# A diffusion block on one core: the row root and the feature gemv at the kernel's front, rearranged

## The chip, the cores and the metric

The kernel runs on one core of one Trainium2 chip. The metric is the device time of one execution in microseconds. Before the change the median of three runs is 1590.12 us (1589.61 to 1594.4).

## What is computed

One block of a diffusion backbone works on 256 latent tokens `x` and 256 context tokens `ctx`, each with 2048 features, in float32:

```python
lam = exp(sum(lp[0] * lp[1])) - exp(sum(lp[2] * lp[3])) + lam_init      # lp = da_lambda
mod   = silu(c) @ w_ada + b_ada         # latent: shift, scale, gate, twice
mod_c = silu(c_ctx) @ w_ada + b_ada     # context
h_lat = rmsnorm(x, norm1_g) * (1 + sc1) + sh1
h_ctx = rmsnorm(ctx, norm1_g) * (1 + csc1) + csh1
dq, dk, dv, cq, ckv, kr, ga, gb = split(h @ w_in)     # for h_lat and h_ctx
# differential attention (uses lam) and latent attention over 512 keys,
# their output projections, sigmoid gates, w_out, gated residual
# second norm and modulation, SwiGLU (2048 -> 5632 -> 2048), gated residual, final norm
```

## The kernel before

Matmul operands are split into a high and a low part (`fp32r`), and each product is three matmuls: high by high, low rows by high weights, high rows by low weights. ScalarE makes the high part of a weight tile (`wh`, L169), VectorE the low part (`wl`, L170); both kinds of tile share rings of three buffers, the raw tiles a ring of five.

The first stage, which the change touches, does this. `xnT` holds the 512 tokens as columns and the features in 16 k-tiles of 128. Eight transfers on SyncE's queue bring it. ScalarE squares each tile of 1024 columns (L320, L323), VectorE adds the squares into `xsum` (L324, seven adds), then adds its two halves (L325), and one matmul with a matrix of ones sums over the partitions (L327, into `ps`). `newton` (L305 to L312) makes the reciprocal root of the 512 sums: Ln, Exp and Square on ScalarE, three steps on VectorE. The result `rb` scales each k-tile of `xnT` (L370).

The shift and the scale of the first norm come from `w_mod`, the first two chunks of `w_ada`. `mod_gemv(f0, nf, order)` computes them for `nf` k-tiles of output features from `f0` on: SyncE loads `w_mod` in tiles of 512 KB (`sraw`, 12 buffers; four tiles for one k-tile, eight for two), 16 matmuls of 32 columns each, four of them side by side in the array, go into `pgb` (L390), ScalarE copies it to `res` (L383), TensorE transposes it (L386), VectorE reduces it to the columns `modc` (L397 to L404), and then the k-tiles' modulated rows are made: high part on ScalarE (L409), low part on VectorE (L410, L411). Behind that, `first_group(k0, nk)` loads the k-tiles' share of 832 columns of `w_in` (the MLA key and value compression, the rope key, and the first four heads' pairs of `dk`), splits it, and puts 42 feature matmuls for each k-tile into a `queue`: 7 banks (`g0`, numbers 0 to 6), six each.

Within `tc.manual_schedule` TensorE's order is the program's. The list `order` writes it: `"g4"` is four matmuls of the gemv, a number takes so many feature matmuls from the queue, `"t"` is the copy, eight feature matmuls and the transposes. On the other engines the framework's planner orders the instructions. The calls are

```python
mod_gemv(0, 1, ["g4", "g4", "g4", "g4", "t"])
mod_gemv(1, 1, [16, "g16", "t"])
mod_gemv(2, 2, [36, "g8", 4, "g8", "t"])
for f0 in range(4, KT, 2):
    mod_gemv(f0, 2, [len(queue) - 54, "g16", "t", 22])
pop(len(queue))
```

The last block's matmuls go bank by bank (0, 1, 5, 2, 3, 4, 6), all others go over the k-tiles with the banks in two parts (2, 3, 5 and 0, 1, 4, 6). Then the banks are evacuated: 0, 1, 4 and 6 are `dk` of the first four heads (`evac_dk`, rotary positions and split, VectorE L530 to L540), 2, 3 and 5 the MLA latents (`evac_latent`), while TensorE goes on with `dq` and `dv`. Banks 4 and 6 are read by the second pair of heads.

The lambdas (L273 to L287) stand ahead of all that: a transfer of 128 KB on ScalarE's queue into a buffer of the `wl` ring, two multiply-reduce steps, an Exp and two small steps. Their result `nlam` is read by the differential attention (L665).

Of the kernel before, what the change touches and what calls it, by code (L numbers as in the profile page):

```python
# [11 lines left out]
F32 = mybir.dt.float32  # L12
# [84 lines left out]
def kernel(  # L97
# [41 lines left out]
    def nm(s):  # L139
        uid[0] += 1  # L140
        return f"{s}{uid[0]}"
# [17 lines left out]
    def load_w(src, a, n):  # L159
        raw = stream.tile([P, 1024], F32, tag="raw", name=nm("raw"), bufs=5)  # L160
        nc.sync.dma_start(out=raw[:, : a * n], in_=src)
        return raw[:, : a * n].rearrange("p (a n) -> p a n", a=a)
# [54 lines left out]
    def group_b(w, c0, n, nkt, toks, name, ups=2, tick=None, stagger=0):  # L217
# [52 lines left out]
    b1 = const.tile([P, 16], F32, name="b1")  # L270
    nc.vector.tensor_scalar_add(b1, bcol[:, 16:32], 1.0)

    ls = const.tile([P, 4], F32, name="ls")  # L273
    setup = stream.tile([P, 1024], F32, tag="wl", name="setup", bufs=3)
    lamb, lj = setup[:, 0:256], setup[:, 512:576]
    nc.scalar.dma_start(
        out=lamb, in_=da_lambda.rearrange("a f d -> (a f d)").partition_broadcast(P))
    for i in range(2):
        nc.vector.tensor_tensor_reduce(
            lj, lamb[:, i * 128 : i * 128 + 64], lamb[:, i * 128 + 64 : i * 128 + 128],  # L280
            op0=ALU.mult, op1=ALU.add, scale=1.0, scalar=0.0, accum_out=ls[:, i : i + 1])
    with tc.issue_after(silu.ins):
        nc.scalar.preload_act_table_set("natural_log_exp_and_others")
    nc.scalar.activation(ls[:, 0:2], ls[:, 0:2], AF.Exp)
    nlam = ls[:, 2:3]
    nc.vector.tensor_sub(nlam, ls[:, 1:2], ls[:, 0:1])
    nc.vector.tensor_scalar_add(nlam, nlam, -LAM_INIT)  # L287


    right, close_right = pool("right", side="right")  # L290
# [4 lines left out]
    xnT = xp.tile([P, KT, 512], F32, name="xnT")  # L295
    c32 = xp.tile([P, KT, 32], F32, name="c32")
    nc.gpsimd.memset(c32, 0.0)
    nc.vector.tensor_copy(c32[:, :, 0:2], cols[:, 0:32].rearrange("p (v k) -> p k v", v=2))
    srp, close_sr = pool("srp", side="right")

# [4 lines left out]
    def newton(y, q, ps, n):  # L305

        nc.scalar.activation(y, ps, AF.Ln, bias=epsc, scale=1.0 / n)
        nc.scalar.activation(y, y, AF.Exp, scale=-0.5)
        nc.scalar.activation(q, y, AF.Square)
        nc.vector.scalar_tensor_tensor(q, ps, n * EPS, q, op0=ALU.add, op1=ALU.mult)  # L310
        nc.vector.tensor_scalar(q, q, -0.5 / n, 1.5, op0=ALU.mult, op1=ALU.add)
        nc.vector.tensor_mul(y, y, q)  # L312

    xsum = xp.tile([P, 1024], F32, name="xsum")
    for u in range(8):
        xu = xnT[:, 2 * u : 2 * u + 2, :]
        nc.sync.dma_start(out=xu, in_=xt[:, 2 * u : 2 * u + 2, :])
        xu = xu.rearrange("p a n -> p (a n)")
        if u == 0:
            nc.scalar.activation(xsum, xu, AF.Square)  # L320
        else:
            sq = stream.tile([P, 1024], F32, tag="wh", name=nm("sq"), bufs=3)
            nc.scalar.activation(sq, xu, AF.Square)  # L323
            nc.vector.tensor_add(xsum, xsum, sq)  # L324
    nc.vector.tensor_add(xsum[:, :512], xsum[:, :512], xsum[:, 512:])  # L325
    ps = acc(nm("ps"))
    nc.tensor.matmul(ps, ones, xsum[:, :512], start=True, stop=True)  # L327
    rb = xsum[:, :512]
    newton(rb, xsum[:, 512:], ps, D)

# [32 lines left out]
    def mod_gemv(f0, nf, order):  # L365

        for kt in range(f0, f0 + nf):
            nc.vector.tensor_mul(xnT[:, kt, :], xnT[:, kt, :], rb)  # L370
        w = nf * 256
        a = 4 // nf
        vs = []
        for u in range(KT // a):
            raw = srp.tile([P, 1024], F32, tag="sraw", name=nm("sraw"), bufs=SRAW)
            last_load[0] = nc.sync.dma_start(
                out=raw, in_=w_mod.block(u * a, a, f0 * P, nf * P, D + f0 * P, nf * P))
            vs += [raw[:, i * w : (i + 1) * w] for i in range(a)]
        done = 0
        for step in order:  # L380
            if step == "t":
                res = xp.tile([P, 512], F32, tag="res", name=nm("res"), bufs=1)
                nc.scalar.copy(res[:, :w], pgb[:, :w])  # L383
                pop(8)
                for j in range(2 * nf):
                    nc.tensor.transpose(pgb[:, j * P : (j + 1) * P], res[:, j * P : (j + 1) * P], ident)  # L386
            elif isinstance(step, str):
                for kt in range(done, done + int(step[1:])):
                    j = kt % 4
                    nc.tensor.matmul(pgb[32 * j : 32 * j + 32, :w], c32[:, kt, :], vs[kt],  # L390
                                     start=kt < 4, stop=kt >= 12, tile_position=(0, 32 * j))
                done += int(step[1:])
            else:
                pop(step)
        assert done == KT

        nc.vector.tensor_reduce(  # L397
            modr[:, :, :nf, :],
            pgb[:, : 2 * nf * P].rearrange("p (s i g v) -> p s i v g", s=2, i=nf, g=4)[:, :, :, 0:2, :],
            axis=AX.X, op=ALU.add)  # L400
        for i in range(nf):
            kt = f0 + i
            nc.vector.tensor_scalar(modc[:, kt, 0, :], modr[:, 0, i, :], bcol[:, kt : kt + 1], None, op0=ALU.add)
            nc.vector.tensor_scalar(modc[:, kt, 1, :], modr[:, 1, i, :], b1[:, kt : kt + 1],  # L404
                                    n1g[:, kt : kt + 1], op0=ALU.add, op1=ALU.mult)
            for v, hh in enumerate((hl, hc)):
                sh, sc = modc[:, kt, 0, v : v + 1], modc[:, kt, 1, v : v + 1]
                xv = xnT[:, kt, v * 256 : v * 256 + 256]
                nc.scalar.activation(hh[0][:, kt, :], xv, AF.Identity, bias=sh, scale=sc)  # L409
                nc.vector.tensor_scalar(xv, xv, sc, sh, op0=ALU.mult, op1=ALU.add)  # L410
                nc.vector.tensor_sub(hh[1][:, kt, :], xv, hh[0][:, kt, :].bitcast(F32))  # L411
        queue.extend(first_group(f0, nf))

    def first_group(k0, nk):

        v = load_w(w_in.block(k0, nk, 3584, 320), nk, 320)
        wh = stream.tile([P, 1024], F32R, tag="wh", name=nm("wh"), bufs=3)
        wl = stream.tile([P, 1024], F32R, tag="wl", name=nm("wl"), bufs=3)
        h1 = wh[:, : nk * 384].rearrange("p (a n) -> p a n", a=nk)
# [2 lines left out]
        nc.vector.tensor_sub(l1[:, :, :320], v, h1[:, :, :320].bitcast(F32))  # L422
        nc.scalar.copy(h1[:, :, 320:], h1[:, :, 256:320].bitcast(F32))
        nc.scalar.copy(l1[:, :, 320:], l1[:, :, 256:320].bitcast(F32))
        h2, l2 = split_w(load_w(w_in.block(k0, nk, 1024, 512), nk, 512), nk, 512)

        def cut(i, n):
            return (h1, l1)[i][:, :, n * P : (n + 1) * P] if n < 3 else (h2, l2)[i][:, :, (n - 3) * P : (n - 2) * P]
# [27 lines left out]
        return todo  # L456

    with tc.manual_schedule(engines={mybir.EngineType.PE}):
        mod_gemv(0, 1, ["g4", "g4", "g4", "g4", "t"])
        mod_gemv(1, 1, [16, "g16", "t"])  # L460
        mod_gemv(2, 2, [36, "g8", 4, "g8", "t"])
        for f0 in range(4, KT, 2):

            mod_gemv(f0, 2, [len(queue) - 54, "g16", "t", 22])
        pop(len(queue))
    with tc.issue_after(last_load[0].ins):
        nc.sync.dma_start(out=cst, in_=consts)
    close_sr()
# [541 lines left out]
```

## Time and profile before

| | |
|---|---|
| median of 3 runs | 1590.12 us (1589.61 to 1594.4) |
| profiled execution | 1599.08 us, its span 1597.3 us |
| TensorE, matmuls | 1541.9 us busy (97%) |
| VectorE | 1016.4 us (64%) |
| ScalarE | 737.4 us (46%) |
| GpSimd | 16.1 us (1%) |
| HBM read | 352.37 MB, 222 GB/s over the span |

The rows are of one execution taken by the hardware profiler. Times are microseconds from the start of the span unless marked ns. PE is TensorE, PEld its weight loads, DVE VectorE, ACT ScalarE, POOL GpSimd, SP SyncE; L327 is line 327 of the kernel. A window's row gives busy time and instructions of PE, PEld, DVE, ACT and POOL in that order, then the granted TensorE clock as a share of full speed (2.4 GHz), the busy share of the 16 DMA engines and the GB/s that they moved. A float32 matmul stands as two records. A matmul's end in the records includes the time until its result is out, so matmuls that follow each other overlap a little.

### The profile page before, as it was taken

The page shows a single profiled execution, that of the slowest core. Times are in us where ns is not written, and L with a number is a line of the kernel's source. Part 1 is how long each engine was busy: PE and PEld are TensorE (multiplying, and loading weights), DVE is VectorE, ACT ScalarE, POOL GpSimd, SP SyncE. Part 2 cuts the span into 40 slices and gives each one's busy share as a digit, 9 for nine tenths or more (in the row PEclk, how much of TensorE's full clock was granted, in tenths as well). Part 3 has the DMA queues.
Part 4 walks back from the last instruction along what each step waited for, and adds up shares of the span by engine and source line. Part 5 has one row for each costly group of instructions (what it writes and reads, how often), then busy time and mean ns, then how long its engine had stood idle before and what let it go on. Part 6 is the DMA issues. An engine that isn't in the chain of part 4 may idle for free.

```text
span 1597.3 us, 28864 instructions
## 1 busy us (share of the span) xinstructions
PE 1541.9 (97%) x11966; PEld 1445.0 (90%) x11966; DVE 1016.4 (64%) x1360; ACT 737.4 (46%) x1038; POOL 16.1 (1%) x14
## 2 busy tenths in 40 slices
PE   3899999998999999999999999999999999999997
PEld 2678899997889999999999999999999999888886
DVE  5437887787896667666776566767554554445454
ACT  4335455545675443444445444444444444344343
POOL 0000000000000000000000000000000000011010
PEclk9999999999999999999999999999999999999999
DMA  9894653456455787888884678888565656655663
GB/s 369 338 367 153 213 170 121 136 178 197 142 165 170 257 290 249 280 269 292 306 280 159 205 229 281 282 285 272 196 194 192 196 194 219 194 190 191 193 191 119
DMA packets 100594, 356.34 MB, mean 223 GB/s; under 512 B 10992, under 2 KB 13552, under 8 KB 100208
## 3 DMA queue, kind: packets, MB, share of 16 engines
q1 hardware_dynamic: 99600, 351.58, 65.9%
q10 hardware_dynamic: 864, 2.93, 0.6%
q8 instruction: 93, 1.52, 0.4%
q14 instruction: 37, 0.30, 0.1%
HBM read 352.37 MB, written 2.10 MB: 222 GB/s over the span
## 4 chain that ended last, share of the span: by engine, by line
PE 72%; DMA 9%; DVE 6%; issue 1%; ACT 1%; DVEq 0%; POOLq 0%; POOL 0%; ACTq 0%; SPq 0%
PE up L157 15%; PE down L157 15%; PE gate L157 13%; DMA raw<-in_w_ada_dram 9%; PE dv L157 4%; PE wo L157 4%; PE ga L157 3%; PE gb L157 3%; PE yab L157 3%; DVE gacc L489 3%; PE dk L157 2%; PE dq L157 1%; PE cq L157 1%; DVE wl L170 1%; PE pt L629 1%
## 5 line engine op out<-in xcount | busy, mean ns | idle before, releaser
L170 DVE TENSOR_TENSOR wl<-raw,wh 128x1024 fp32r<-128x1024 f32 (+1 forms) x453 | 549.4, 1222 | 335.5 <-ACT wh L169 319.5
L169 ACT CAST wh<-raw 128x1024 fp32r<-128x1024 f32 (+1 forms) x453 | 474.8, 1051 | 580.0 <-PE down L157 137.1
L489 DVE SCALAR_TENSOR_TENSOR gacc<-raw,cols,gacc 128x1024 f32<-128x1024 f32 x120 | 154.0, 1283 | 124.4 <-DMA raw<-in_w_ada_dram 124.0
L157 PE MATMUL gate<-h,wh 128*128 128x256 f32 x1386 | 176.4, 278 | 0.0
L157 PE MATMUL up<-h,wh 128*128 128x256 f32 x1386 | 176.1, 277 | 0.0
L157 PE MATMUL down<-wh,hid 128*128 128x512 f32 x696 | 174.5, 391 | 0.0
L157 PEld LDWEIGHTS gate<-h,wh 128*128 128x128 f32 x1386 | 167.1, 188 | 0.4 <-DVE h L885 0.2
L157 PEld LDWEIGHTS up<-h,wh 128*128 128x128 f32 x1386 | 166.8, 188 | 0.0
L157 PEld LDWEIGHTS down<-wh,hid 128*128 128x128 f32 x696 | 130.7, 188 | 28.9
L157 PE MATMUL gate<-h,wl 128*128 128x256 f32 x704 | 97.0, 278 | 0.2 <-DVE wl L170 0.2
L157 PE MATMUL up<-h,wl 128*128 128x256 f32 x704 | 96.8, 277 | 0.0
L157 PE MATMUL down<-wl,hid 128*128 128x512 f32 x352 | 95.6, 392 | 0.0
L157 PEld LDWEIGHTS gate<-h,wl 128*128 128x128 f32 x704 | 88.0, 188 | 0.4 <-DVE wl L170 0.4
L157 PEld LDWEIGHTS up<-h,wl 128*128 128x128 f32 x704 | 87.9, 188 | 0.0
L157 PEld LDWEIGHTS down<-wl,hid 128*128 128x128 f32 x352 | 66.1, 188 | 14.1
L157 PE MATMUL ga<-hl,wh 128*128 128x256 f32 x504 | 66.9, 282 | 0.0
L157 PE MATMUL gb<-hl,wh 128*128 128x256 f32 x504 | 64.4, 278 | 0.0
L157 PE MATMUL wo<-mT,wh 128*128 128x256 f32 x504 | 63.9, 277 | 0.0
L157 PEld LDWEIGHTS ga<-hl,wh 128*128 128x128 f32 x504 | 62.6, 192 | 0.6 <-ACT wh L169 0.4
L157 PEld LDWEIGHTS gb<-hl,wh 128*128 128x128 f32 x504 | 60.9, 188 | 0.4 <-ACT wh L169 0.4
L157 PEld LDWEIGHTS wo<-mT,wh 128*128 128x128 f32 x504 | 60.3, 188 | 0.4 <-issue 0.4
L390 PE MATMUL pgb<-sraw,c 128*32 128x512 f32 (+1 forms) x288 | 32.6, 595 | 17.6 <-DMA sraw<-in_w_mod_dram 17.6
(334 smaller groups left out, 2315.2 us busy)
## 6 DMA issues: line engine op xcount, KB each, us to landing
raw<-in_w_ada_dram SPq DMA_DIRECT2D x128, 512.0 KB, 4.4
raw<-in_w_in_dram SPq DMA_DIRECT2D x119, 512.0 KB, 4.6
raw<-in_w_ffn_gate_dram SPq DMA_DIRECT2D x88, 512.0 KB, 4.3
raw<-in_w_ffn_up_dram SPq DMA_DIRECT2D x88, 512.0 KB, 4.4
raw<-in_w_ffn_down_dram SPq DMA_DIRECT2D x88, 512.0 KB, 4.2
sraw<-in_w_mod_dram SPq DMA_DIRECT2D x64, 512.0 KB, 8.8
raw<-in_w_out_dram SPq DMA_DIRECT2D x32, 512.0 KB, 5.0
raw<-in_w_o_da_dram SPq DMA_DIRECT2D x16, 512.0 KB, 4.8
```

The source lines that it names most:

```text
L157: nc.tensor.matmul(region, lhsT, rhs, start=False, stop=last, skip_group_check=key != self.lead)
L169: nc.scalar.copy(h, v)
L170: nc.vector.tensor_sub(l, v, h.bitcast(F32))
L390: nc.tensor.matmul(pgb[32 * j : 32 * j + 32, :w], c32[:, kt, :], vs[kt], start=kt < 4, stop=kt >= 12, tile_position=(0, 32 * j))
L489: nc.vector.scalar_tensor_tensor(a, raw, cols[:, kt : kt + 1], a, op0=ALU.mult, op1=ALU.add)
L629: nc.tensor.transpose(pt[:, j * P : (j + 1) * P], a[:, j * P : (j + 1) * P], ident)
```

## The change

The lambdas become a function that is called behind the first stage. The last square stays in its own tile: `row_sums` halves both tiles, sums them with two matmuls, and makes the root in two halves of 256 columns, each of which scales the first k-tile at once. `row_sums` is now a step (`"r"`) in TensorE's written order, between the second and the third four gemv matmuls. `"d13"` and the like are matmuls of the ones with a cleared tile `warm` into a bank that is not in use yet; their result is not used. The first k-tile's two `w_in` loads are issued ahead of its `w_mod` loads. The numbers in the order of the first three calls change, and the last block of two k-tiles becomes two blocks of one.

```diff
@@ -270,21 +270,23 @@
     b1 = const.tile([P, 16], F32, name="b1")
     nc.vector.tensor_scalar_add(b1, bcol[:, 16:32], 1.0)
-    ls = const.tile([P, 4], F32, name="ls")
-    setup = stream.tile([P, 1024], F32, tag="wl", name="setup", bufs=3)
-    lamb, lj = setup[:, 0:256], setup[:, 512:576]
-    nc.scalar.dma_start(
-        out=lamb, in_=da_lambda.rearrange("a f d -> (a f d)").partition_broadcast(P))
-    for i in range(2):
-        nc.vector.tensor_tensor_reduce(
-            lj, lamb[:, i * 128 : i * 128 + 64], lamb[:, i * 128 + 64 : i * 128 + 128],
-            op0=ALU.mult, op1=ALU.add, scale=1.0, scalar=0.0, accum_out=ls[:, i : i + 1])
     with tc.issue_after(silu.ins):
         nc.scalar.preload_act_table_set("natural_log_exp_and_others")
-    nc.scalar.activation(ls[:, 0:2], ls[:, 0:2], AF.Exp)
+    ls = const.tile([P, 4], F32, name="ls")
     nlam = ls[:, 2:3]
-    nc.vector.tensor_sub(nlam, ls[:, 1:2], ls[:, 0:1])
-    nc.vector.tensor_scalar_add(nlam, nlam, -LAM_INIT)
+
+    def lambdas():
+        setup = stream.tile([P, 1024], F32, tag="wl", name="setup", bufs=3)
+        lamb, lj = setup[:, 0:256], setup[:, 512:576]
+        nc.scalar.dma_start(
+            out=lamb, in_=da_lambda.rearrange("a f d -> (a f d)").partition_broadcast(P))
+        for i in range(2):
+            nc.vector.tensor_tensor_reduce(
+                lj, lamb[:, i * 128 : i * 128 + 64], lamb[:, i * 128 + 64 : i * 128 + 128],
+                op0=ALU.mult, op1=ALU.add, scale=1.0, scalar=0.0, accum_out=ls[:, i : i + 1])
+        nc.scalar.activation(ls[:, 0:2], ls[:, 0:2], AF.Exp)
+        nc.vector.tensor_sub(nlam, ls[:, 1:2], ls[:, 0:1])
+        nc.vector.tensor_scalar_add(nlam, nlam, -LAM_INIT)
     right, close_right = pool("right", side="right")
@@ -295,6 +297,8 @@
     xnT = xp.tile([P, KT, 512], F32, name="xnT")
     c32 = xp.tile([P, KT, 32], F32, name="c32")
     nc.gpsimd.memset(c32, 0.0)
+    warm = xp.tile([P, 512], F32, name="warm")
+    nc.gpsimd.memset(warm, 0.0)
     nc.vector.tensor_copy(c32[:, :, 0:2], cols[:, 0:32].rearrange("p (v k) -> p k v", v=2))
     srp, close_sr = pool("srp", side="right")
@@ -319,14 +323,22 @@
         if u == 0:
             nc.scalar.activation(xsum, xu, AF.Square)
         else:
-            sq = stream.tile([P, 1024], F32, tag="wh", name=nm("sq"), bufs=3)
-            nc.scalar.activation(sq, xu, AF.Square)
-            nc.vector.tensor_add(xsum, xsum, sq)
-    nc.vector.tensor_add(xsum[:, :512], xsum[:, :512], xsum[:, 512:])
+            xsq = stream.tile([P, 1024], F32, tag="wh", name=nm("sq"), bufs=3)
+            nc.scalar.activation(xsq, xu, AF.Square)
+            if u < 7:
+                nc.vector.tensor_add(xsum, xsum, xsq)
     ps = acc(nm("ps"))
-    nc.tensor.matmul(ps, ones, xsum[:, :512], start=True, stop=True)
     rb = xsum[:, :512]
-    newton(rb, xsum[:, 512:], ps, D)
+
+    def row_sums():
+
+        for i, src in enumerate((xsum, xsq)):
+            nc.vector.tensor_add(src[:, :512], src[:, :512], src[:, 512:])
+            nc.tensor.matmul(ps, ones, src[:, :512], start=i == 0, stop=i == 1)
+        for v in range(2):
+            cs = slice(v * 256, v * 256 + 256)
+            newton(rb[:, cs], xsum[:, 512 + v * 256 : 768 + v * 256], ps[:, cs], D)
+            nc.vector.tensor_mul(xnT[:, 0, cs], xnT[:, 0, cs], rb[:, cs])
@@ -366,8 +378,16 @@
-        for kt in range(f0, f0 + nf):
-            nc.vector.tensor_mul(xnT[:, kt, :], xnT[:, kt, :], rb)
+
+
+        def scaled():
+            for kt in range(f0, f0 + nf):
+                nc.vector.tensor_mul(xnT[:, kt, :], xnT[:, kt, :], rb)
+
+        if f0:
+            scaled()
+        else:
+            raws = first_loads(f0, nf)
         w = nf * 256
         a = 4 // nf
         vs = []
@@ -384,6 +404,11 @@
                 pop(8)
                 for j in range(2 * nf):
                     nc.tensor.transpose(pgb[:, j * P : (j + 1) * P], res[:, j * P : (j + 1) * P], ident)
+            elif step == "r":
+                row_sums()
+            elif isinstance(step, str) and step[0] == "d":
+                for _ in range(int(step[1:])):
+                    nc.tensor.matmul(g0[6].t, ones, warm, start=True, stop=True)
             elif isinstance(step, str):
                 for kt in range(done, done + int(step[1:])):
                     j = kt % 4
@@ -409,11 +434,15 @@
                 nc.scalar.activation(hh[0][:, kt, :], xv, AF.Identity, bias=sh, scale=sc)
                 nc.vector.tensor_scalar(xv, xv, sc, sh, op0=ALU.mult, op1=ALU.add)
                 nc.vector.tensor_sub(hh[1][:, kt, :], xv, hh[0][:, kt, :].bitcast(F32))
-        queue.extend(first_group(f0, nf))
-
-    def first_group(k0, nk):
-
-        v = load_w(w_in.block(k0, nk, 3584, 320), nk, 320)
+        queue.extend(first_group(f0, nf, first_loads(f0, nf) if f0 else raws))
+
+    def first_loads(k0, nk):
+        return (load_w(w_in.block(k0, nk, 3584, 320), nk, 320),
+                load_w(w_in.block(k0, nk, 1024, 512), nk, 512))
+
+    def first_group(k0, nk, raws):
+
+        v = raws[0]
         wh = stream.tile([P, 1024], F32R, tag="wh", name=nm("wh"), bufs=3)
         wl = stream.tile([P, 1024], F32R, tag="wl", name=nm("wl"), bufs=3)
         h1 = wh[:, : nk * 384].rearrange("p (a n) -> p a n", a=nk)
@@ -422,7 +451,7 @@
         nc.vector.tensor_sub(l1[:, :, :320], v, h1[:, :, :320].bitcast(F32))
         nc.scalar.copy(h1[:, :, 320:], h1[:, :, 256:320].bitcast(F32))
         nc.scalar.copy(l1[:, :, 320:], l1[:, :, 256:320].bitcast(F32))
-        h2, l2 = split_w(load_w(w_in.block(k0, nk, 1024, 512), nk, 512), nk, 512)
+        h2, l2 = split_w(raws[1], nk, 512)
         def cut(i, n):
             return (h1, l1)[i][:, :, n * P : (n + 1) * P] if n < 3 else (h2, l2)[i][:, :, (n - 3) * P : (n - 2) * P]
@@ -456,13 +485,16 @@
         return todo
     with tc.manual_schedule(engines={mybir.EngineType.PE}):
-        mod_gemv(0, 1, ["g4", "g4", "g4", "g4", "t"])
-        mod_gemv(1, 1, [16, "g16", "t"])
-        mod_gemv(2, 2, [36, "g8", 4, "g8", "t"])
-        for f0 in range(4, KT, 2):
+        mod_gemv(0, 1, ["d13", "g4", "d1", "g4", "r", "g4", "d1", "g4", "t", "d3"])
+        mod_gemv(1, 1, [20, "g16", "t"])
+        mod_gemv(2, 2, [22, "g8", 6, "g8", "t"])
+        for f0 in range(4, KT - 2, 2):
             mod_gemv(f0, 2, [len(queue) - 54, "g16", "t", 22])
+        mod_gemv(KT - 2, 1, [len(queue) - 54, "g16", "t", 22])
+        mod_gemv(KT - 1, 1, [len(queue) - 54, "g16", "t"])
         pop(len(queue))
+    lambdas()
     with tc.issue_after(last_load[0].ins):
         nc.sync.dma_start(out=cst, in_=consts)
     close_sr()
```

## Rows read from the trace of the kernel before

**Rows 1.** The page, busy time by engine.

```profile
PE 1541.9 (97%) x11966; PEld 1445.0 (90%) x11966; DVE 1016.4 (64%) x1360; ACT 737.4 (46%) x1038; POOL 16.1 (1%) x14
```

**Rows 2.** Wide windows: start:end, length, busy us (x instructions) by engine, clock, DMA.

```profile
0.00:60.00 60.00, 31.68 (x232) 20.60 (x236) 32.97 (x72) 22.93 (x38) 0.73 (x5) 0.94 0.94 363
60.00:140.00 80.00, 80.00 (x692) 64.06 (x684) 32.82 (x91) 29.53 (x55) 0.00 (x0) 1.00 0.87 326
140.00:165.00 25.00, 22.70 (x182) 21.15 (x182) 24.18 (x55) 15.90 (x30) 0.00 (x0) 1.00 0.16 47
```

**Rows 3.** Finer windows of the first 37 us, same columns.

```profile
0.00:5.00 5.00, 0.00 (x0) 0.00 (x0) 0.18 (x3) 1.28 (x1) 0.73 (x5) 1.00 0.65 205
5.00:8.00 3.00, 0.00 (x0) 0.00 (x0) 0.23 (x2) 1.51 (x2) 0.00 (x0) 1.00 0.73 219
8.00:30.00 22.00, 6.71 (x37) 2.13 (x37) 14.46 (x26) 12.63 (x20) 0.00 (x0) 1.00 1.03 409
30.03:36.85 6.82, 5.81 (x39) 4.44 (x43) 5.90 (x12) 1.26 (x4) 0.00 (x0) 0.50 1.03 410
```

**Rows 4.** Timeline of the front: start, us, engine, line, operation [idle before, releaser].

```profile
5.28 1.28 ACT L283 ACT_TABLE_LOAD   x1
...
9.26 1.04 ACT L320 ACTIVATE xsum<-xnT 128x1024 f32<-128x1024 f32 x1
...
11.28 9.20 DVE L324 TENSOR_TENSOR xsum<-xsum,sq 128x1024 f32<-128x1024 f32 x7 [1.54 <-ACT sq L323]
...
17.59 1.08 PE L390 MATMUL pgb<-sraw,c 128*32 128x256 f32 x8 [17.59 <-DMA sraw<-in_w_mod_dram]
...
21.25 2.08 PE L327 MATMUL ps<-xsum,ones 128*128 128x512 f32 x2 [2.59 <-DVE xsum L325]
...
24.75 0.63 ACT L309 ACTIVATE xsum<-xsum 128x512 f32<-128x512 f32 x1
...
29.50 0.38 PE L155 MATMUL g<-hl,wh 128*128 128x256 f32 x1 [2.50 <-ACT hl L409]
...
31.04 0.58 PE L157 MATMUL g<-hl,wh 128*128 128x256 f32 x1 [1.16 <-DVE hl L411]
...
34.53 3.05 PE L390 MATMUL pgb<-sraw,c 128*32 128x256 f32 x32
...
58.93 1.49 PE L390 MATMUL pgb<-sraw,c 128*32 128x512 f32 x12
```

**Rows 5.** Timeline of TensorE at the stage's end.

```profile
119.25 0.60 PE L386 MATMUL pgb<-cols,res 128*128 128x128 f32 x4
...
128.41 3.64 PE L390 MATMUL pgb<-sraw,c 128*32 128x512 f32 x32
...
133.04 0.60 PE L386 MATMUL pgb<-cols,res 128*128 128x128 f32 x4
...
148.53 1.88 PE L572 MATMUL pq<-t,ones 128*128 128x512 f32 x4
...
163.47 1.20 PE L157 MATMUL dq<-hl,wl 128*128 128x256 f32 x8 [1.38 <-DVE wl L170]
```

**Rows 6.** SyncE's queue, 0 to 160 us: line, waited for, total us, times, longest.

```profile
SPq L376 <- DMA setup<-in_da_lambda_dram: 2.5, 1, 2.5
```

**Rows 7.** TensorE's waits, 0 to 160 us, same columns.

```profile
PE g L157 <- DVE hl L411: 3.7, 3, 1.3
```

**Rows 8.** Timeline of VectorE at the stage's end.

```profile
139.77 1.23 DVE L170 TENSOR_TENSOR wl<-raw,wh 128x1024 fp32r<-128x1024 f32 x1
...
140.92 0.45 DVE L537 STREAM_SHUFFLE r<-g 128x256 f32<-128x256 f32 x1
...
154.03 1.23 DVE L170 TENSOR_TENSOR wl<-raw,wh 128x1024 fp32r<-128x1024 f32 x1
...
161.74 0.42 DVE L530 TENSOR_TENSOR dk<-r,dk 64x256 fp32r<-64x256 f32 x1
```

**Rows 9.** Timeline of VectorE, one later wait for a transfer.

```profile
187.56 1.28 DVE L489 SCALAR_TENSOR_TENSOR gacc<-raw,cols,gacc 128x1024 f32<-128x1024 f32 x1 [5.10 <-DMA raw<-in_w_ada_dram]
```

## Prediction

> **What bounds the kernel now.** I read the page first: TensorE is busy for 97% of the span [rows 1], so only what idles or slows TensorE can shorten it. The wide windows say where that is: TensorE is busy for 31.7 of the first 60 us and for all 80 from there to 140 [rows 2]. So the change is worth what it brings in the first 60 us, if TensorE stays the pacer behind that. Finer windows add the clock: half (1.2 GHz) from 30.03 to 36.85 us, full (2.4 GHz) behind [rows 3]. Before 30 us they print 1.00, but the row-sum matmul at 21.25 takes 2.08 us, and two of the same shape (two records each) at 148.53, with the clock full, take 1.88 [rows 4, 5]: the front runs at half clock too.
>
> Then the timeline of the first 60 us, followed backward. TensorE's first feature matmul starts at 29.50, its second (which needs the low part of the rows) at 31.04. Ahead of them stands the row root from 23.33, ahead of that VectorE's seven adds (9.20 us from 11.28, so 1.31 each), a halving add, and the row-sum matmul. The first square starts at 9.26, although the table load that it follows ended at 6.56: the lambdas' Exp stood in front of it [rows 4]. SyncE waited 2.5 us for the lambdas' transfer [rows 6], and while that ran (5 to 8 us) the queues moved 219 GB/s, against 409 behind [rows 3].
>
> Last the stage's end. Each block of two k-tiles takes 13.8 us from transposes to transposes; at 163.47 TensorE waits 1.38 us for a weight split (L170) [rows 5], and VectorE is busy for 24.2 of 25 us from 140 to 165 [rows 2]. So behind 140 us TensorE and VectorE are nearly level.
>
> **The change, step by step.**
>
> *Lambdas out of the front.* The first square may start at 6.56, 2.7 us earlier. The adds then start at 8.6; there are six (7.9 us), to 16.5; two halving adds, half as wide (0.7 each), end at 17.2 and 17.9, against 21.2 now. The transfers: those 3 us fell short by 570 KB, 1.4 us at 410 GB/s, and the lambdas' own 131 KB are 0.3. The first gemv tile, here at 17.59, comes 1.7 us earlier, but 1.0 later for the two w_in loads (426 KB) now issued ahead of it: 16.9. Its followers come every 1.28 us (524 KB at 410): 18.2, 19.4, 20.7. If the dip has another cause, all are 1.4 us later.
>
> The Trainium skill (DMA: Bandwidth & Descriptors, Queues, rings and completion order) says each DMA engine alternates between its queues packet by packet; by that the lambdas would cost no more than their share, 0.3 us, and the front would gain 1.4 us less. The rows of 5 to 8 us speak against it; the rival on the transfers has its price.
>
> *Idle matmuls.* 18 in all, each of the row-sum matmul's shape: 2.0 at half clock, 0.94 at full [rows 4, 5]. The clock rose at 36.85, 5.8 us after TensorE began to work without pause at 31.04; I take three slow ones. From 1.8 us (POOL's memsets end by about 1.3, one of 0.5 is added [rows 3]): 3 x 2.0 + 10 x 0.94 ends at 17.2, about when the first gemv tile is there. Bounds: none slow, 14.0; all slow, 27.8.
>
> *TensorE's order then.* Four gemv matmuls (0.5, half of the 1.08 for four now) to 17.7; one idle to 18.6; four to 19.1; the row sums, now two matmuls, 2 x 0.94 to 21.0. VectorE's halves are there by 17.9. Now: 23.33. The remaining gemv, an idle one, the copy and the transposes end at 23.8, three idle ones at 26.6.
>
> *Root in halves.* ScalarE's three steps take some 0.63 each for 512 columns [rows 4]; I take 0.4 for a half (0.32 if it were all streaming). Second half done: 21.0 + 6 x 0.4 + four VectorE steps of some 0.4 = 25.0. By then the modulation columns are nearly there (transposes at 23.8), and one ScalarE step of 0.6 later the first feature matmul could start, at 26.0; the idle ones hold it to 26.6. The second comes 1.54 behind the 26.0, as now: 27.5, **3.5 us** earlier than 31.04.
>
> *Full clock.* The 13 feature matmuls between 31.04 and 34.4 follow each other at 0.21 and fall to 0.113 (the last block's 84 in 9.5 us): **1.3**; the second gemv (3.05) falls to half of 3.64: **1.2** [rows 4, 5]. There and at the next k-tiles TensorE waits for VectorE's low parts, 3.7 us in three waits [rows 7]. With 20, 22 and 6 for 16, 36 and 4, the second of them has 14 feature matmuls in front of it, not 18 (0.113 each: 0.45 lost), the third 20, not 12 (0.9 gained): **0.5**. Front in sum: **6.5 us**; from 3 (dip stays, part of the clock) to 8.5 (those waits gone too).
>
> *Does the queue keep up?* A block needs eight w_mod tiles and two w_in tiles, 5.05 MB, 12.3 us at 410 GB/s, under 13.8. The tightest is the block of k-tiles 4 and 5. Up to its last tile it is 18.7 MB (rows and columns 4.4, 24 tiles of 0.524, w_in 1.7), of which 1.0 is there in the first 5 us: 5 + 17.7 / 0.41 = 48, its gemv at 58.93 - 6.5 = 52.4 [rows 3, 4]. Held, by 4 us.
>
> *Last two blocks of one k-tile.* TensorE's work is the same (two half-wide gemvs of 1.8 for one of 3.64). The stage's end moves from 148.5 to 142.0. But bank 0 is now complete 72 matmuls of 0.113 (8.2 us) before that end, then only 36 (4.1): at 138.1. Its evacuation, which started at 140.92, starts 2.8 us earlier, not 6.5. The lambdas' VectorE steps (six short ones, 0.9 in all, the gap between 8.6 and 9.7 us now) now fall into that full stretch, and they take a wl buffer of the three, so that the split at 139.77 (1.23), here ahead of the evacuation, falls behind it. In the order of now the wait that ends at 163.47 would be over only 2.8 - 0.9 - 1.2 = **0.7 us** earlier. On the other side nothing is returned, 6.5, if the splits go ahead of the dk evacuations of banks 4 and 6, which only the second pair of heads reads. The trace shows a split put there already (154.03, ahead of dk steps that run to 162 [rows 8]), so I take two thirds of the way: 4.6 kept. The lambdas' ScalarE share (issue 0.45, Exp 0.2) lies beside this; ScalarE has gaps there. Were VectorE to stand in front of their transfer, up to 5.1 more, as with the w_ada tile at 187.56 [rows 9].
>
> **Sum.** The profiled execution took 1599.1 (span 1597.3 and 1.8 around it) and would take 1594.5; that is 9 above the median of the runs, 1590.1, and I take the difference to lie in stages that the change leaves alone: **1585.5 us**.
>
> **Rivals.** (1) All is kept: 6 to 9, 1581 to 1584. For it: VectorE has 5.1 us of idle time at 182 [rows 9], and TensorE's wait there is short. Against: at 163 TensorE is the one that waits. (2) VectorE sets the time and the front's gain is returned: 0.7 kept, about 1589.4. For it: VectorE's full stretch [rows 2]. (3) The dip at 5 to 8 us is not the lambdas': 1.4 less, 1586.9; against it, full rate from the microsecond in which their transfer landed. (4) Slower: the idle matmuls do not raise the clock. 13 end at 27.8, with the gemv, an idle one and the row sums at 2.0 or 1.0 the sums end at 36, the last three at 47, 17 us behind 29.50: about 1607. It decides once some six of the 18 run slow beyond my three (1.06 each against 6.5). Against it: gemv and feature matmuls with less work each raised the clock at 36.85. The Trainium skill (TensorE: Matmul & The Clock Gate, Seeing it yourself) reports a gate stuck low for over 50 us; no run here shows that.
>
> **Chances.** Part kept, 1583.5 to 1587.5: 0.46 (0.12 of it rival 3), split evenly by the line of 0.3% (4.8 us, 1585.3), about what can be told from no change. All kept: 0.25. All returned: 0.17. Slower, 0.12: the clock 0.07, VectorE stopped by the lambdas' transfer 0.05. So faster 0.48, same 0.40, slower 0.12. The range for 8 in 10 takes in most of both neighbours, 1580 to 1592.5; the likeliest alone has 1583.5 to 1587.5.
>
> **What would show it.** First square near 6.6; no dip at 5 to 8 us; idle matmuls of under 1 us from 8 us on, clock full and through 60; row sums done near 21, first feature matmul near 26; wide gemv of k-tiles 4 and 5 near 52; stage's last matmul near 142; then longer waits for L170 up to 165. I am wrong if the stage ends within 2 us of 148.5, if the first 13 idle matmuls end behind 19 us, or if TensorE crosses 142 to 165 with no more idle time than now.

## The result, and the profile after

The changed kernel is slower: 1606.03 us in the median (1605.22 to 1608.96, four runs) against 1591.62 (four runs) for the kernel before, a ratio of 1.0086 (95% interval 1.006 to 1.0111). I had forecast 1585.5. The profiled execution took 1608.96, its span 1607.2, 9.9 us more than the span before.

Busy time on the page, to be read beside [rows 1]:

```profile
PE 1559.1 (97%) x12036; PEld 1452.1 (90%) x12036; DVE 1017.1 (63%) x1367; ACT 739.0 (46%) x1046; POOL 16.6 (1%) x15
```

TensorE has 17 us more of busy time (the idle matmuls alone are 13.55 of it up to 15.3 us) and is still at 97%: the page alone shows no loss. The windows do (columns as in [rows 2]):

```profile
0.00:60.00 60.00, 52.28 (x298) 28.77 (x298) 32.48 (x70) 24.58 (x42) 1.19 (x6) 0.94 0.97 371
5.00:8.00 3.00, 3.00 (x7) 1.23 (x6) 0.42 (x3) 2.83 (x4) 0.00 (x0) 1.00 1.03 419
30.00:34.00 4.00, 4.00 (x37) 3.03 (x39) 3.60 (x7) 0.86 (x2) 0.00 (x0) 0.58 1.03 408
40.00:44.00 4.00, 4.00 (x22) 1.44 (x21) 1.21 (x2) 0.00 (x0) 0.00 (x0) 0.57 0.80 309
140.00:165.00 25.00, 15.02 (x104) 13.66 (x104) 23.02 (x59) 15.73 (x31) 0.00 (x0) 0.83 0.22 69
156.00:166.00 10.00, 4.29 (x20) 4.29 (x21) 9.66 (x19) 3.84 (x8) 0.00 (x0) 0.51 0.28 77
190.00:200.00 10.00, 5.28 (x42) 4.90 (x41) 4.32 (x8) 3.05 (x8) 0.00 (x0) 0.86 0.42 133
200.00:205.00 5.00, 4.87 (x22) 4.54 (x23) 3.72 (x7) 2.42 (x6) 0.00 (x0) 0.59 0.45 161
```

From 140 to 165 us TensorE is busy for 15.0 of 25 us, where it had 22.7 [rows 2], and from 156 to 166 its clock is at half (0.51, 1.2 GHz). VectorE is nearly as full there as before (23.0 and 24.2). The front looks as hoped: 419 GB/s from 5 to 8 us against 219 [rows 3]. Its timeline, beside [rows 4]:

```profile
1.77 13.55 PE L411 MATMUL g_x<-warm,ones 128*128 128x512 f32 x26 [1.77 <-POOL warm L301]
...
6.69 1.06 ACT L324 ACTIVATE xsum<-xnT 128x1024 f32<-128x1024 f32 x1
...
16.50 0.64 PE L415 MATMUL pgb<-sraw,c 128*32 128x256 f32 x8 [1.18 <-DMA sraw<-in_w_mod_dram]
...
19.66 1.02 PE L337 MATMUL ps<-sq,ones 128*128 128x512 f32 x2
...
25.82 0.68 PE L155 MATMUL g<-hl,wh 128*128 128x256 f32 x1
26.35 0.38 PE L157 MATMUL g<-hl,wh 128*128 128x256 f32 x1
27.32 0.38 PE L157 MATMUL g<-hc,wh 128*128 128x256 f32 x1 [0.59 <-ACT hc L434]
29.15 0.38 PE L157 MATMUL g<-hc,wh 128*128 128x256 f32 x1 [1.44 <-DVE hc L436]
```

The second feature matmul starts at 26.35 (31.04 before), but then TensorE waits for the context rows' parts, until 29.15. Now VectorE and TensorE at the stage's end, beside [rows 8] and [rows 5], and one later row of TensorE:

```profile
138.26 0.68 DVE L170 TENSOR_TENSOR wl<-raw,wh 128x512 fp32r<-128x512 f32 x1
141.04 0.01 DVE L569 LOAD_MASK_SELECT r<-g  x1 [2.10 <-PE g L157]
...
143.44 0.23 DVE L284 CUSTOM_DVE_ANT_0 setup<-setup 128x64 f32<-128x64 f32 x1 [0.19 <-DMA setup<-in_da_lambda_dram]
...
148.17 1.22 DVE L170 TENSOR_TENSOR wl<-raw,wh 128x1024 fp32r<-128x1024 f32 x1
...
160.44 1.22 DVE L170 TENSOR_TENSOR wl<-raw,wh 128x1024 fp32r<-128x1024 f32 x1
```

```profile
144.92 1.88 PE L604 MATMUL pq<-t,ones 128*128 128x512 f32 x4
...
149.44 1.21 PE L157 MATMUL dq<-hl,wl 128*128 128x256 f32 x8 [0.80 <-DVE wl L170]
150.49 2.05 PE L157 MATMUL dq<-hl,wh 128*128 128x256 f32 x16
161.71 2.08 PE L157 MATMUL dq<-hl,wl 128*128 128x256 f32 x8 [9.18 <-DVE wl L170]
163.59 3.37 PE L157 MATMUL dq<-hl,wh 128*128 128x256 f32 x16
166.80 1.07 PE L157 MATMUL dq<-hl,wl 128*128 128x256 f32 x8
167.71 1.98 PE L157 MATMUL dq<-hl,wh 128*128 128x256 f32 x16
...
200.13 0.80 PE L690 MATMUL ps<-dk,dq 128*128 128x512 f32 x1 [4.85 <-ACT t L656]
```

The first stage's last matmul (`pq`) comes at 144.92, 3.6 us earlier. VectorE then stands idle for 2.10 us until bank 0 is complete, just where the kernel before made the `dq` split of 139.77. That split now comes at 148.17, the second at 160.44 instead of 154.03, and TensorE waits 9.18 us for it. The second split waits for nothing that the rows show: ScalarE had made its high part by 146.33, and VectorE is busy for 18.6 of the 19.4 us between the start of the evacuation (141.04) and the split. It stands behind that work in VectorE's order; before, 12.6 us of work stood there (140.92 to 154.03). TensorE comes out of the wait at half clock: eight matmuls in 2.08 us and sixteen in 3.37, where the next ones take 1.07 and 1.98.

The count up to the attention's fifth matmul, the first that waits, which starts at 200.13 (192.11 before, behind a wait of 2.17 us): 3.6 gained; the waits for `dq` splits are 10.0 us in all against 1.7, 8.3 lost; 2.4 lost at half clock; 2.7 more of waiting ahead of the attention itself. That makes 9.8 lost, against 8.0 in the trace; 1.8 came back somewhere that I didn't trace. Half clock from 200 to 205 us (4.87 us busy at 0.59) adds 2.0, and the span 9.9 is there: behind it nothing is gained or lost between these two profiles. The medians differ by 14.4, since the profiled execution before was 9 us over its median and this one 3; what moves the later stages by that much from run to run stays open.

### The profile page after: what moved, and what is told of

Read it like the earlier page. It is cut to its first block, busy times and chain, and to the rows that moved or that the text cites. A ratio compares the mean times of both kernels' runs of the same rounds, so it can differ in the third digit from the quotient of the medians.

```text
span 1607.2 us, 29029 instructions
## 1 busy us (share of the span) xinstructions
PE 1559.1 (97%) x12036; PEld 1452.1 (90%) x12036; DVE 1017.1 (63%) x1367; ACT 739.0 (46%) x1046; POOL 16.6 (1%) x15
## 4 chain that ended last, share of the span: by engine, by line
PE 76%; DMA 10%; DVE 9%; issue 2%; ACT 1%; DVEq 0%; POOLq 0%; POOL 0%; ACTq 0%
PE down L157 15%; PE up L157 13%; PE gate L157 11%; DMA raw<-in_w_ada_dram 10%; PE gb L157 4%; PE ga L157 4%; PE g L157 4%; PE dv L157 3%; PE yab L157 3%; DVE gacc L521 3%; DVE wl L170 2%; PE wo L157 2%; PE dk L157 2%; PE dq L157 2%; PE pgb L415 2%
## 5 line engine op out<-in xcount | busy, mean ns | idle before, releaser
L157 PE MATMUL g<-hc,wh 128*128 128x256 f32 x192 | 39.5, 286 | 2.0 <-DVE hc L436 1.4
```

What stands on the lines that cost most here:

```text
L157: nc.tensor.matmul(region, lhsT, rhs, start=False, stop=last, skip_group_check=key != self.lead)
```

## The experiments

All ratios are to the kernel before on the same chip, with a 95% interval; the runs were on several chips, so kernels are compared by ratios, not by times. *pq* is the start of the stage's last matmul, *dq wait* the longest wait of TensorE for a `dq` split, *cq* the first matmul behind the four pairs of heads of the differential attention, all in the profiled execution, in us.

| kernel | ratio | pq | dq wait | cq |
|---|---|---|---|---|
| before | 1 | 148.5 | 1.4 | 364.4 |
| after | 1.0086 [1.006, 1.0111] | 144.9 | 9.2 | 374.8 |
| lambdas at the front | 1.0118 [1.0083, 1.0153] | 147.1 | 11.1 | 377.8 |
| last block of two k-tiles | 1.0059 [1.0036, 1.0081] | 143.2 | 4.0, 3.2 | 372.4 |
| both of these | 1.0007 [0.998, 1.0033] | 145.6 | 1.4 | 360.0 |
| before, last block halved | 1.0126 [1.0053, 1.0199] | 148.6 | 11.1 | 378.1 |
| k-tile 15 in other buffers | 1.0025 [1.0002, 1.0049] | 144.7 | 1.2 | 361.5 |
| the same, lambdas late | 1.0015 [0.9994, 1.0036] | 146.0 | 1.7 | 364.9 |
| two k-tiles, lambdas in another ring | 0.9965 [0.9944, 0.9987] | 142.0 | 1.3 | 357.0 |
| **two k-tiles, lambdas late** | 0.9966 [0.9946, 0.9986] | 143.8 | 1.4 | 357.5 |
| that, short cover | 1.002 [1.0002, 1.0038] | 142.0 | 8.4 | 364.3 |
| that, no idle matmuls | 0.9968 [0.9946, 0.9989] | 143.9 | 1.4 | 359.2 |
| that, whole root | 0.9971 [0.994, 1.0001] | 142.4 | 1.4 | 357.1 |
| before, lambdas late | 0.9989 [0.9969, 1.0008] | 146.3 | 1.4 | 361.6 |

The dq wait and cq order the kernels nearly as the ratios do; pq does not.

**Which part loses.** Theory A: the two blocks of one k-tile leave the evacuation too little cover. B: the lambdas' place does it. C: VectorE sets the time, and any gain of the front is returned.

*Lambdas back at the front, all else as changed.*

```diff
+    lambdas()
...
         pop(len(queue))
-    lambdas()
```

> The changed kernel with the lambdas back at the front (their transfer, two reduces, Exp and two small steps ahead of the squares), all else as changed. Theory A (the two last blocks of one k-tile leave the evacuation too little cover): little comes back, 1600 to 1607 us, and TensorE still waits 8 us or more for the first dq splits behind the stage. Theory B (the lambdas' place in the wl ring and their VectorE steps delay the dq splits): 1588 to 1594. Theory C (VectorE paces 140 to 180 us, so any gain of the front is returned): about 1592.

Measured 1611.93, above what any of the three had, with one wait of 11.1 us: B alone is out.

*Last block of two k-tiles again, the lambdas where the change put them.*

```diff
-        for f0 in range(4, KT - 2, 2):
+        for f0 in range(4, KT, 2):
             mod_gemv(f0, 2, [len(queue) - 54, "g16", "t", 22])
-        mod_gemv(KT - 2, 1, [len(queue) - 54, "g16", "t", 22])
-        mod_gemv(KT - 1, 1, [len(queue) - 54, "g16", "t"])
```

> The changed kernel with the last block again of two k-tiles, lambdas still behind the stage. Theory A: 1583 to 1590 us, evacuation begins 7 to 8 us before the stage's last matmul. Theory B: 1600 to 1607, since the split of the first dq unit still stands behind the evacuation. Theory C: about 1592.

Measured 1601.57, the time of B, with two waits of 3.2 and 4.0 us: some of the loss stays, so A alone is out too.

*Both edits.*

> The changed kernel with both undone: lambdas at the front, last block of two k-tiles; what stays is the root in two halves, the idle matmuls, the early w_in loads and the new counts. Theories A and B: the stage's end comes 2 to 4 us earlier and stays earlier, 1586 to 1590 us. Theory C: 1591 to 1593, TensorE's waits for L170 longer by what the front gained.

Measured 1593.55, ratio 1.0007, no difference from the kernel before, which by the time alone speaks for C. The profile says otherwise: the long waits are gone, pq is 2.9 us earlier (about half of the 5.3 of the run above, since the lambdas stand in front again), and cq is 4.4 us earlier. An interval of 0.5% can't tell that from nothing.

*The kernel before with its last block halved, and nothing else.*

```diff
-        for f0 in range(4, KT, 2):
+        for f0 in range(4, KT - 2, 2):
             mod_gemv(f0, 2, [len(queue) - 54, "g16", "t", 22])
+        mod_gemv(KT - 2, 1, [len(queue) - 54, "g16", "t", 22])
+        mod_gemv(KT - 1, 1, [len(queue) - 54, "g16", "t"])
```

> The kernel before with nothing changed but the last block split in two of one k-tile. Theory A: slower by 6 to 12 us, 1597 to 1603, with a wait of TensorE for L170 of 5 us or more. Theories B and C: 1590 to 1594.

Measured 1613.92, a loss of 1.26% (0.53 to 1.99): this part alone is enough for a loss like the whole change's. The intervals overlap, so that it loses more is not shown.

**Cover or ring.** Two blocks of one k-tile take four buffers of each weight ring of three, where one block takes two, and behind the stage the lambdas take one more. So either bank 0 is complete too late (A1), or the `dq` split finds no buffer ahead of the evacuation (A2).

*The split tiles of k-tile 15 out of the first stage's pool* (shown for the 320 columns; the same for the 512).

```diff
-        wh = stream.tile([P, 1024], F32R, tag="wh", name=nm("wh"), bufs=3)
-        wl = stream.tile([P, 1024], F32R, tag="wl", name=nm("wl"), bufs=3)
+        if k0 == KT - 1:
+            wh = srp.tile([P, 1024], F32R, tag="sraw", name=nm("wh"), bufs=SRAW)
+            wl = srp.tile([P, 1024], F32R, tag="sraw", name=nm("wl"), bufs=SRAW)
+        else:
+            wh = stream.tile([P, 1024], F32R, tag="wh", name=nm("wh"), bufs=3)
+            wl = stream.tile([P, 1024], F32R, tag="wl", name=nm("wl"), bufs=3)
```

> The changed kernel, but the four split tiles of the last one-k-tile block (k-tile 15) come out of the first stage's pool instead of the rings of three, so that both dq splits can go ahead of the evacuation on VectorE again; the banks still complete as late as in the changed kernel, and the lambdas stay where the change put them. Theory A1 (the cover itself is too short: bank 0 complete 36 matmuls ahead of the stage's end): VectorE's evacuation ends as late as before this edit, TensorE's idle time only moves from the wait for the dq split to the waits for the evacuated tiles (dv, the transposes), TensorE busy 140 to 165 still about 15 to 18 us, first dv matmul near 168, time 1603 to 1607. Theory A2 (the rings: two blocks where one was take four buffers of rings of three, so the dq split falls behind the evacuation): no wait of over 2 us for a dq split, first dv matmul about 11 us behind pq as in the kernel before (near 156), clock full through 165, time 1590 to 1594.

Measured 1597.37, between the two theories' times. The timeline of VectorE in this run:

```profile
136.77 1.22 DVE L174 TENSOR_TENSOR wl<-raw,wh 128x1024 fp32r<-128x1024 f32 x1
...
138.83 1.23 DVE L174 TENSOR_TENSOR wl<-raw,wh 128x1024 fp32r<-128x1024 f32 x1
...
140.27 1.23 DVE L174 TENSOR_TENSOR wl<-raw,wh 128x1024 fp32r<-128x1024 f32 x1
141.54 0.75 DVE L527 TENSOR_SCALAR gacc<-raw,cols 128x1024 f32<-128x1024 f32 x1
143.75 0.01 DVE L577 LOAD_MASK_SELECT r<-g  x1 [1.46 <-PE g_x L157]
```

Three `dq` splits stand ahead of the evacuation, no wait for one is over 1.2 us, and 0.6 of the 0.86% are back, although the evacuation starts later than ever: at 143.75, 0.9 us ahead of pq, for it waited for the stage's last feature matmul. (Its tiles probably reuse the memory that k-tile 15 still holds; the rows show only the wait.) So with the splits in front most of the loss goes, even with less cover than in the changed kernel, as A2 had it. This run can't price the cover.

*The same, with the lambdas behind the first pair's dv.*

> The changed kernel with the split tiles of k-tile 15 out of the first stage's pool, as above, and the lambdas behind the first pair's dv: of the change's stage end only the later completion of the banks is left. If the cover is the cause (A1): 1600 to 1605, with first dv matmul over 18 us behind pq. If the order of the dq splits is (A2, and the lambdas by the same ring): 1587 to 1591, first dv matmul 10 to 13 us behind pq.

Measured 1594.77: again between the two theories' times, with the same late start of the evacuation (145.07). The first dv matmul comes at 158.86, 12.9 us behind pq, where A2 had 10 to 13 and A1 over 18.

*Last block of two k-tiles, the lambdas in place but in another ring* (their call stands a few lines further down, where that ring exists).

```diff
-        setup = stream.tile([P, 1024], F32, tag="wl", name="setup", bufs=3)
-        lamb, lj = setup[:, 0:256], setup[:, 512:576]
+        setup = t512("setup")
+        lamb, lj = setup[:, 0:256], setup[:, 256:320]
```

> The changed kernel with a last block of two k-tiles, and the lambdas computed at the same place as in the changed kernel but in a buffer of another ring than the low parts of the weights (the ring of the evacuation's temporaries). If the lambdas hurt by the buffer that they take from the ring of three: the dq split goes ahead of the evacuation again, wait for it at most 2 us, first dv matmul about 10 us behind pq as in the variant with both parts undone, time 1588 to 1593. If they hurt by VectorE's 0.9 us and their order in the full stretch: the wait stays near 7 us and the time near 1601.

Measured 1588.7, ratio 0.9965 against 1.0059 with the buffer of the `wl` ring. VectorE now makes the six short steps from 132.65 on, ahead of the `dq` split (133.29) and of the evacuation; with the buffer of the `wl` ring it made them within the evacuation (from 136.94), and the first `dq` split came at 148.86. The steps cost nothing that these runs can tell; the buffer, with the order that came with it, costs about 0.9%.

*Last block of two k-tiles, the lambdas behind the first pair's dv.*

```diff
         dv = evac_dv(group_b(w_in, 2048 + p * 256, 256, KT, TOKS4, "dv", ups=4, tick=tick))
+        if p == 0:
+            lambdas()
```

> The changed kernel with a last block of two k-tiles, and the lambdas computed only behind the first pair's dv, just ahead of the first attention: the front is the changed kernel's, the stage's end the kernel before's. Stage's last matmul near 143, the wait for the dq split at most 2 us, first dv matmul near 153, 5 us ahead of the kernel before. If TensorE then stays the pacer (theory A): 1585 to 1588, the best version. If VectorE and the w_ada transfers pace the stretch from 140 to 200 (theory C): the 5 us are returned by 205 us and the time is 1589 to 1592.

Measured 1587.4 (12 runs) against 1593.38 (35 runs): faster than both kernels. VectorE at the stage's end:

```profile
134.73 1.23 DVE L170 TENSOR_TENSOR wl<-raw,wh 128x1024 fp32r<-128x1024 f32 x1
135.88 0.01 DVE L566 LOAD_MASK_SELECT r<-g  x1
...
149.04 1.23 DVE L170 TENSOR_TENSOR wl<-raw,wh 128x1024 fp32r<-128x1024 f32 x1
```

TensorE:

```profile
153.17 0.28 PE L155 MATMUL dv<-wh,hl 128*128 128x256 f32 x1
...
158.48 1.20 PE L157 MATMUL dq<-hl,wl 128*128 128x256 f32 x8 [1.38 <-DVE wl L170]
```

The window:

```profile
140.00:165.00 25.00, 23.05 (x184) 21.55 (x183) 24.28 (x51) 14.70 (x26) 0.00 (x0) 1.00 0.28 87
```

The split is directly ahead of the evacuation, as at 139.77 and 140.92 before [rows 8], and the 4.7 us of pq are still there at cq (6.9): nothing is returned, and theory C is out.

*That version with the cover cut short*: gemvs, number of tiles and transfers stay, only the order of the last 84 matmuls becomes that of two blocks.

```diff
-            for m in (0, 1, 5, 2, 3, 4, 6):
-                for a in range(nk):
+            for a in range(nk):
+                for m in (0, 1, 5, 2, 3, 4, 6):
                     one(m, a)
```

> The best version so far (the changed kernel with a last block of two k-tiles and the lambdas behind the first pair's dv), with the last block's 84 feature matmuls in another order: k-tile 14 for all seven banks, then k-tile 15 for all seven, as two blocks of one k-tile would have them. Bank 0 is then complete 36 matmuls ahead of the stage's end, not 72; gemvs, rings, transfers and the dq split's place ahead of the evacuation stay. If the short cover is what is left of the loss once the rings are put right: first dq matmul 2 to 3 us behind pq instead of 1.3, first dv matmul 12 to 14 us behind pq instead of 9.4, time 1593 to 1597. If the cover costs nothing and the halved gemvs and their waits are what is left: first dv matmul under 11 us behind pq, time 1586 to 1589.

Measured 1594.74: 0.5% lost by the order alone. The time is the one expected of a short cover, but the way there is not: the first `dq` matmul follows pq by 1.4 us, and the loss is one long wait again. VectorE, TensorE and the window:

```profile
133.17 1.23 DVE L170 TENSOR_TENSOR wl<-raw,wh 128x1024 fp32r<-128x1024 f32 x1
...
137.98 0.01 DVE L566 LOAD_MASK_SELECT r<-g  x1 [3.59 <-PE g L157]
...
153.40 1.29 DVE L559 TENSOR_TENSOR ckvn<-t,ckvn 128x512 fp32r<-128x512 f32 x2
...
155.62 1.22 DVE L170 TENSOR_TENSOR wl<-raw,wh 128x1024 fp32r<-128x1024 f32 x1
```

```profile
156.90 2.07 PE L157 MATMUL dq<-hl,wl 128*128 128x256 f32 x8 [8.42 <-DVE wl L170]
...
165.12 0.28 PE L155 MATMUL dv<-wh,hl 128*128 128x256 f32 x1
```

```profile
140.00:165.00 25.00, 16.58 (x118) 15.43 (x117) 24.20 (x50) 15.03 (x29) 0.00 (x0) 0.80 0.22 67
```

VectorE stands idle for 3.59 us until bank 0 is complete; the first split is ahead of the evacuation, but the second, at 149.04 in the version above, comes at 155.62. Only 2.1 of these 6.6 us are the later start of the evacuation (137.98 against 135.88). The rest is another order: the MLA latents (`ckvn`) now stand ahead of the second split, and VectorE's work between the start of the evacuation and that split is 17.0 us, not 12.7. TensorE's order changed as well: above, `dv` begins at 153.17, ahead of a `dq` part that waits for a split (158.48); here it comes behind all of `dq` (165.12). So the order written in the program ends with the first stage, where the `manual_schedule` block closes; behind it the planner orders TensorE too. Why it orders so stays open. (The low parts of the 320 columns are here in use up to 12 matmuls ahead of the stage's end, not 24; at 0.113 us each they are free by 141.1 in both runs, so it is not they that hold the second split.) The cover and the ring cost in the same place: a `dq` split gets a later place on VectorE, and TensorE, which does not leave the order that it was given, waits for it.

**What the front is worth.** On the best version, one part taken out, or one part alone on the kernel before.

*No idle matmuls.*

```diff
-        mod_gemv(0, 1, ["d13", "g4", "d1", "g4", "r", "g4", "d1", "g4", "t", "d3"])
+        mod_gemv(0, 1, ["g4", "g4", "r", "g4", "g4", "t"])
```

> The best version so far (the changed kernel with a last block of two k-tiles and the lambdas behind the first pair's dv), with its 18 idle matmuls left out of the first gemv. If they buy the full clock as the prediction's sum had it (1.3 for the feature matmuls, 1.2 for the wide gemv, and the gemvs and row sums ahead of them at full clock): the clock stays half up to about 33 us, the stage's last matmul comes 2.5 to 5 us later, near 147, the time 1590 to 1593. If the lambdas' place alone brings the front's gain: stage's last matmul within 1 us of 143.8, time 1586 to 1589.

Measured 1589.73, the same ratio as with them (0.9968 and 0.9966, each to 0.2%, so 2.5 us would not show in it), pq 143.9 and 143.8.

*Root in one piece.*

```diff
-        for v in range(2):
-            cs = slice(v * 256, v * 256 + 256)
-            newton(rb[:, cs], xsum[:, 512 + v * 256 : 768 + v * 256], ps[:, cs], D)
+        for v in range(1):
+            cs = slice(0, 512)
+            newton(rb[:, cs], xsum[:, 512:], ps[:, cs], D)
```

> The best version so far with the row root in one piece of 512 columns, as in the kernel before. By the prediction's widths the halves bring the first feature matmul about 1 us forward: here it is at 26.8 or later, the context rows' parts may come earlier, since they are not behind a second root: the third and fourth feature matmuls wait less. Stage's last matmul 143 to 145, time 1587 to 1589; if the halves cost more than they bring (seven more steps of fixed length), stage's last matmul under 143.

Measured 1587.96: no difference that the runs can tell. The first two feature matmuls come at 26.64 and 28.19 instead of 25.72 and 26.25, but from there TensorE goes on without a wait, while with halves it is stopped until 29.05. The halves bring forward what then waits for the context rows.

*The lambdas late, alone, on the kernel before*: their lines become the function of the changed kernel.

```diff
         dv = evac_dv(group_b(w_in, 2048 + p * 256, 256, KT, TOKS4, "dv", ups=4, tick=tick))
+        if p == 0:
+            lambdas()
```

> The kernel before with one edit: the lambdas behind the first pair's dv. If their transfer is what cut the front's transfers at 5 to 8 us and held the first square: first square near 6.6, no dip at 5 to 8 us, first feature matmul 1.5 to 3 us earlier than 29.50, stage's last matmul 145.5 to 147, the stage's end unchanged, time 0.1 to 0.2% below the kernel before. If the dip is not theirs, the dip stays and the stage's last matmul is within 1 us of 148.5.

Measured 1592.06, not told apart from the kernel before, but the front moves as expected (ScalarE, then the window):

```profile
6.55 1.06 ACT L322 ACTIVATE xsum<-xnT 128x1024 f32<-128x1024 f32 x1
```

```profile
5.00:8.00 3.00, 0.00 (x0) 0.00 (x0) 0.42 (x3) 2.97 (x4) 0.00 (x0) 1.00 1.02 416
```

The dip is gone, and pq is 2.2 us earlier: of the front's parts that were tried this is the one that shows by itself. The early `w_in` loads and the new numbers in the order were not tried alone.

## Why the prediction was wrong, by its steps

**The step that failed is the last of the sum: "two thirds of the way".** It named the right events: bank 0 complete 36 matmuls ahead of the end, the lambdas' buffer in the `wl` ring, the split of 139.77 falling behind the evacuation. It priced that split at its own length, 1.2 us, in VectorE's order of before, and took 0.7 us as the least and 4.6 as the likely part that would be kept; between the two profiles 9.9 us are lost. The price is that of everything that then stands ahead of the splits on VectorE: the first came 8.4 us later (148.17), the next 6.4 later (160.44), behind 18.6 us of work where 12.6 had stood, and TensorE, which keeps to its order, waited 9.2 us behind a split that takes 1.2. The row that the two thirds leaned on (154.03, ahead of `dk` steps) belonged to an order of VectorE that the change itself altered. Two costs were in no term: the half clock behind the wait (2.4 us, then 2.0 from 200), and a second stop of VectorE for a `w_ada` tile (5.68 us, up to 196.72; before there was one such stop there [rows 9]). The rival "all returned" was closest in mechanism, but it ended at no change; none of the slower rivals was this one. The halved blocks alone (1.26% on the kernel before, interval 0.53 to 1.99), their cover alone (0.54% on the best version) and the lambdas' buffer alone (0.9%) each do it; together, and with the front's gain, they leave 0.86%: they are ways to the same late split, and don't add up.

**The front held.** First square 6.69 (forecast 6.56), row sums done 20.7 (21.0), first feature matmul 25.82 (26.0 to 26.6), second 26.35 (27.5), idle matmuls done 15.3 (17.2; three were taken as slow at 2.0 us and ten at 0.94, lengths that include a tail, while at full clock they follow each other every 0.86 us, and about two and a half were slow). Where the clock did not fall between 30 and 44 us, the wide gemv of k-tiles 4 and 5 starts at 52.46 and 52.84 and pq at 142.0 and 142.4 (the lambdas in another ring, the whole root), against 52.4 and 142.0 of the sum. In the changed kernel they are 55.51 and 144.92: the clock was at half in two stretches. That the front's sum came out is in part luck. TensorE went on without a stop only from 29.15, 1.9 us ahead of 31.04 and not 3.5, since the context rows' parts, which the sum did not name, came late; which other term brought more is not taken apart.

**The dip was the lambdas' transfer**, so that rival is out: with nothing but the lambdas moved the rate is 416 GB/s. The Trainium skill (DMA: Bandwidth & Descriptors, Queues, rings and completion order) states that each DMA engine alternates between its queues packet by packet; the share of 0.3 us that I had worked out from it doesn't account for 219 GB/s over 3 us. Why one small transfer to all partitions costs so much was not tried.

**The idle matmuls do raise the clock**, so the rival at 1607 us is out, though its time came true. But they don't hold it: with the same matmuls up to 29 us the clock fell at about 30 in three profiles (after and both with k-tile 15 in other buffers: 0.58 to 0.60 from 30 to 34), between 37 and 44 in two (the last block of two k-tiles, and the best version: 0.76 over that window), and stayed at 1.00 there in two (the lambdas in another ring, the short cover). What decides it is open. The Trainium skill (TensorE: Matmul & The Clock Gate, Part 1: The HAM clock gate) says that the number of slow matmuls differs between runs of one kernel; these profiles agree: the first 13 idle matmuls took 12.86 to 14.36 us in the eight with the same front. The 2.5 us that I put down to full clock are, in the run without idle matmuls, 0.1 against a profile in which the clock fell once, and 1.5 to 1.9 against those in which it didn't.

**The queue kept up**, as forecast: where the clock held, the gemv of k-tiles 4 and 5 was in time to 0.4 us.

## What to carry to other kernels

Where each engine keeps to an order and a planner makes that order, the price of an instruction that slips is not its own length but the length of all that gets ahead of it: ask what in-order work stands between its old place and its new one, and don't take the other instructions' order as given. Before a step takes a buffer from a ring, count the ring's users up to the next critical one; here 0.9 us of moved work cost nothing that could be told, and the same work with a buffer of the weight ring 0.9%. And split a block only if what becomes ready late by it has nothing behind it: the last block's order is the cover of the next stage.

## What the runs showed of the hardware

A wait of TensorE costs more than its length: out of waits of 8.4 to 11.1 us it came at half clock each time (eight matmuls in 2.07 or 2.08 us against 1.07 to 1.2), and stayed there for some microseconds of work. After the shorter waits of 3.2 and 4.0 us (last block of two k-tiles, the lambdas where the change put them) the next sixteen matmuls took 3.50 and 3.62 us against 1.98: half clock too. With a transfer of 128 KB to all partitions beside the bulk loads the queues moved 219 to 235 GB/s from 5 to 8 us (four profiles), without it 416 to 422 (ten).
